# The order of a trunk kernel's last small operations, of its first casts and transposes, and of one low part of weights

## The chip, the cores and the metric

The kernel runs on one core of one Trainium2 chip. The metric is the time of one execution in microseconds (us) on the device. Five engines work in the core, each through its own list of instructions in order: TensorE (PE in the profile), VectorE (DVE), ScalarE (ACT), GpSimd (POOL) and SyncE (SP), which here only issues transfers.

## The reference, cut to what matters

One layer of a decoder trunk over 512 positions of 1024 values, all float32:

```python
u = rmsnorm(x, ln1_g)
proj = u @ w_in                                  # q, k, v, pool_in, z, xbc, dt, gates
y_a = dilated_attention_mixer(q, k, v, rel_bias) @ w_a
y_b = pool_mixer(pool_in, pool_w, pool_scale) @ w_b
y_c = ssd_mixer(z, xbc, dt, ...) @ w_c
x = x + (gates[0] * y_a + gates[1] * y_b + gates[2] * y_c) @ w_o
x = x + conv_ffn(rmsnorm(x, ln2_g), w_up, conv_w, conv_b, w_down)
return rmsnorm(x, final_g)
```

## The kernel before, in words

Matrix products are made from two parts of each operand, each in the type fp32r: a high part, which is a cast of the value, and a low part, which is the value less its high part. A product is three passes of matmuls: high by high, high by low and low by high. So each block of weights (`raw`) that has come from memory needs a cast into `wh` (ACT, `cast`, L195) and a subtraction into `wl` (DVE, `low`, L217) before its last pass. Weights come as a list of jobs. While job n is multiplied, `prepare` makes the low parts of job n+1, casts job n+2 and fetches job n+3. Every engine's order is the order in which the Python text issues its instructions.

Rows (positions) are kept in four blocks of 128, `tb` 0 to 3. Three places of the program matter here.

**The start.** x arrives in eight pieces, `xin[tb, h]`, h being the half of its 1024 values. `turned(tb)` (L1902) turns the eight 128x128 blocks k of a row block on PE into PSUM; for `tb` 0, 2 and 3 the blocks k and k+4 share a bank. `split_x(tb, k)` then makes `xh[k]` on ACT (L1906) and from it `xl[k]` on DVE (L1907). The first weights, `raw0`, come in two halves of 128 columns, j = 0 and 1. For j = 0 DVE makes the high part `h0` in two casts of 128x512 (L1952), which stand between the second and third `xl` of row block 1; GpSimd then makes the low part `l0` (`low0`, L1886). For j = 1 ACT makes the casts (L1959). On PE stand in a row: `group(0, (HH,))`, high by high for j = 0 over row blocks 0 and 1; `group(0, (HL,))`, with the low parts of x; `group(1, (HH,))`; `turned(2)`; `group(1, (HL,))`; `group(0, (LH,))`, which needs `l0` of j = 0; `turned(3)`; `group(1, (LH,))`, which needs `l0` of j = 1; and then the second half of the columns (all L1918). The build puts one more instruction, shown as `ISA` in the order, on GpSimd ahead of its first operation on two tensors; the profile shows it as two `MODIFY_POOL_CONFIG`.

**The opening of the feed-forward block.** The normed rows of row blocks 2 and 3 are not ready when the up products begin, so the first two up jobs (`opening`, L1560) multiply the first 256 columns alone, and the turns of row blocks 2 and 3 (`late`) lie between. `rest[0]` holds the steps of `prepare` for the first of these jobs: its first `next` makes the low parts of the second job's weights, its second one casts and fetches.

**The end.** `last_group` makes the last down products in seven jobs; the last, "A22", adds one half (512 columns) of row blocks 2 and 3. For each row block, `first` (L1631 on) takes the sum of squares of the half that is done earlier (`ss`) and makes of it the columns `v0` and `vh` on ACT (L1634, L1635). `gamma` multiplies that half by the final weights on DVE (L1641). When the other half has been read from its bank into x (L1694, DVE), `then` takes its sum of squares (ACT, L443) and a root (ACT, L1649), and the generator `rest` makes the norm's factor `rt` in four DVE operations of 128x1 (L1654 to L1657), multiplies both halves (DVE L1662, ACT L1663) and stores them (L1665). `go(tb)` runs `rest` to its next `yield`. The table `order` says which of these calls follow which reading:

```python
("A22", 0): [lambda: gamma(3, 1)],
("A22", 1): [lambda: go(2), lambda: go(2), lambda: go(3), lambda: go(3)]}
```

Of the kernel before, what the change touches and what calls it, by code (L numbers as in the profile page):

```python
# [12 lines left out]
AF = mybir.ActivationFunctionType  # L13
# [3 lines left out]
P = 128  # L17
S = 512
D = 1024
KD = D // P  # L20
# [62 lines left out]
def trunk(ctx: ExitStack, tc, out, x, rel_bias, ln1_g, w_in, b_gate, w_a, pool_w, pool_scale, w_b,  # L83
# [3 lines left out]
    act, dve, pool, pe, sp = nc.scalar, nc.vector, nc.gpsimd, nc.tensor, nc.sync  # L87
# [3 lines left out]
    out = out[0]  # L91
# [17 lines left out]
    def MM(name):  # L109
        return psum.tile([P, S], F32, name=name, tag="mm")  # L110

    def SM(name):
        return psum.tile([P, S], F32, name=name, tag="sm")
# [7 lines left out]
    eps = cpool.tile([P, 1], F32, name="eps")  # L121
# [121 lines left out]
    def chunk_a(ps, ws, j, xh, xl, ks, lo=0, hi=S, k0=0):  # L243
        wh, wl = ws
        mm3(ps[:, lo:hi], lambda k: wh[:, k0 + k, j * P:(j + 1) * P],
            lambda k: wl[:, k0 + k, j * P:(j + 1) * P],
            lambda k: xh(k)[:, lo:hi], lambda k: xl(k)[:, lo:hi], ks)
# [269 lines left out]
    bias = []  # L517
# [769 lines left out]
    COLS = [[cpool.tile([P, 1], F32, name=f"{n}{tb}") for n in ("so", "va", "vo")] for tb in range(4)]  # L1287
# [164 lines left out]
    def up_evac(m, ps):  # L1452
        t = HC[m] = T("hc")
        act.activation(t, ps, AF.Identity, bias=ff["c1"][:, ff["b"] + m:ff["b"] + m + 1], scale=fw(2, m))  # L1454
        for k in range(2):
            sh = 2 - k
            dve.scalar_tensor_tensor(t[:, sh:], ps[:, :S - sh], fw(k, m), t[:, sh:], OP.mult, OP.add)  # L1457
        if m < KF:
            act.activation(t, t, AF.Silu)  # L1459
            return  # L1460
        a = HC[m - KF]
        pool.tensor_tensor(a, a, t, OP.mult)  # L1462

        def later():
            yield
            k = m - KF
            if k % 2:
                h, l = T("fh", F32R), T("fl", F32R)
                act.copy(h, a)
                it = sums_of(HC[k - 1], a, T("sah", F32R), T("sal", F32R),  # L1470
                             lambda j, h, l: FS.__setitem__((j, k // 2), (h, l)), k >= KS)
                next(it)
                dve.tensor_sub(l, a, h.bitcast(F32))
                ACTS[k] = (h, l)
                yield
                for _ in it:
                    yield
                return
            t = T("f0", F32R)
            act.copy(t[:, :256], a[:, :256])  # L1480
            dve.tensor_sub(t[:, 256:], a[:, :256], t[:, :256].bitcast(F32))
            FS[0, k // 2] = (t[:, :256], t[:, 256:])

        running.append(later())
# [61 lines left out]
    def up_jobs():  # L1546
        held, rest = [], []

        def opening(job, half):
            def body(ws):  # L1550
                uh2, ul2 = nxt["uh"], nxt["ul"]
                if half == 0:
                    rest.append(job.prepare(later=True))
                    next(late[1])
                pss = [MM("pu") for _ in range(2)]

                def product(a, b, i):
                    for j in range(2):
                        for k in range(KD):
                            pe.matmul(pss[j][:, :256], a[:, k, j * P:(j + 1) * P], b[:, k, :256],  # L1560
                                      start=i + k == 0, stop=i == 2 and k == KD - 1)

                product(ws[0], uh2, 0)
                product(ws[0], ul2, 1)
                if half == 0:
                    product(ws[1], uh2, 2)
                next(late.pop(0), None)

                next(rest[0], None)
                if half:  # L1570
                    product(ws[1], uh2, 2)
                for j in range(2):
                    held.append((ws, j, pss[j], KF * half + j))
                if half == 0:
                    return
                for n, (ws_, j, ps, m) in enumerate(held):
                    chunk_a(ps, ws_, j, lambda k: uh2[:, k, :], lambda k: ul2[:, k, :], range(KD), 256, S)
                    if n == 1:
                        job.prepare()
                    up_evac(m, ps)  # L1580
                    step()
            return body

        for p in range(KF // 2):
            for half in range(2):
                def body(ws, p=p, half=half):
                    uh2, ul2 = nxt["uh"], nxt["ul"]
                    for j in range(2):
                        ps = MM("pu")
                        chunk_a(ps, ws, j, lambda k: uh2[:, k, :], lambda k: ul2[:, k, :], range(KD))  # L1590
                        up_evac(KF * half + 2 * p + j, ps)
                        step()
                c = half * DFF + p * 256
                job = Job([wsrc(w_up, 0, KD, c, c + 256)], KD, 256, body)
                if p == 0:
                    job.late = True
                    job.body = opening(job, half)
                yield job
# [3 lines left out]
    def last_group():  # L1602
# [22 lines left out]
        def begin():  # L1625
            fin["g"] = grow(final_g)
            act.activation(small("sq", [P, 1]), eps, AF.Sqrt)

        def first(tb, h):
            half = 1 - h  # L1630
            ss, v0, vh = COLS[tb]  # L1631
            xg = T("xg")
            squares(act, X1[tb, half], ss)
            act.activation(v0, ss, AF.Identity, bias=eps, scale=1.0 / D)  # L1634
            act.mul(vh, v0, -0.5)  # L1635
            fin[tb] = xg
            if tb < 2:
                pool.tensor_tensor(xg, X1[tb, half], fin["g"][half], OP.mult)

        def gamma(tb, half):  # L1640
            dve.tensor_tensor(fin[tb], X1[tb, half], fin["g"][half], OP.mult)  # L1641

        def then(tb, h):
            t, g = X1[tb, h], fin["g"]
            _, v0, vh = COLS[tb]
            ss, v, sq, r, rt = (small(n, [P, 1]) for n in ("ss", "v", "sq", "r", "rt"))
            o = {1 - h: fin[tb], h: T("xg")}
            squares(act, t, ss)
            act.activation(sq, ss, AF.Sqrt, bias=v0, scale=1.0 / D)  # L1649
            if tb < 2:  # L1650
                pool.tensor_tensor(o[h], t, g[h], OP.mult)

            def rest():
                dve.scalar_tensor_tensor(v, ss, -0.5 / D, vh, OP.mult, OP.add)  # L1654
                dve.reciprocal(r, sq)
                dve.scalar_tensor_tensor(rt, r, v, r, OP.mult, OP.mult)
                dve.scalar_tensor_tensor(rt, rt, 1.5, r, OP.add, OP.mult)  # L1657
                yield
                if tb < 2:
                    act.mul(o[h], o[h], rt)  # L1660
                else:
                    dve.scalar_tensor_tensor(o[h], t, rt, g[h], OP.mult, OP.mult)  # L1662
                act.mul(o[1 - h], o[1 - h], rt)  # L1663
                for i in (h, 1 - h):
                    (sp if i == h or tb < 3 else act).dma_start(  # L1665
                        out[tb * P:(tb + 1) * P, i * S:(i + 1) * S], o[i])
                yield

            fin["rest", tb] = rest()

        def go(tb):
            next(fin["rest", tb])
# [38 lines left out]
        def three_read(tb, h):  # L1711
            if tb == 0:
# [12 lines left out]
        order = {(2, 1): [lambda: go(0), lambda: go(0)],  # L1725
                 (3, 0): [lambda: go(1), lambda: seven.prepare(), lambda: go(1)],
                 (3, 1): [lambda: gamma(2, 1)],
                 ("A22", 0): [lambda: gamma(3, 1)],
                 ("A22", 1): [lambda: go(2), lambda: go(2), lambda: go(3), lambda: go(3)]}

        def soon():
            four.load = None
# [124 lines left out]
    raw0 = w0.raw = wraw.tile([P, KD, 256], F32, name="raw", tag="raw")  # L1857
# [19 lines left out]
    h0 = w0.high = whp.tile([P, KD, 256], F32R, name="wh", tag="wh")  # L1877
# [3 lines left out]
    def part(j, k0, k1):  # L1881
        return slice(None), slice(k0, k1), slice(j * P, (j + 1) * P)

    def low0(j, k0, k1):
        o = part(j, k0, k1)
        pool.tensor_tensor(l0[o], raw0[o], h0[o].bitcast(F32), OP.subtract)  # L1886
# [11 lines left out]
    def turned(tb):  # L1898
        if tb % 2 == 0:
            banks[:] = [SM("uT") for _ in range(4)]  # L1900
        for k in range(KD):
            pe.transpose(block(tb, k), xin[tb, k // 4][:, (k % 4) * P:(k % 4 + 1) * P], eye)  # L1902

    def split_x(tb, k):
# [31 lines left out]
    ss = small("ss", [P, 8])  # L1936
# [9 lines left out]
    for k in range(KD):  # L1946
        split_x(0, k)
    turned(1)
    for k in range(KD):
        if k == 2:  # L1950
            for k0 in (0, 4):
                dve.tensor_copy(h0[part(0, k0, k0 + 4)], raw0[part(0, k0, k0 + 4)])  # L1952
            low0(0, 0, KD)
        split_x(1, k)
    warm_up(STILL, 0)
    group(0, (HH,), 0, 256)
# [36 lines left out]
    rt, rd = T("rowsT"), dram.tile([S], F32, name="rows")  # L1993
# [86 lines left out]
```

## Time and profile before

| what | value |
|---|---|
| median of three runs | 1012.55 us (1012.4 to 1013.15) |
| the profiled execution | 1012.54 us, its span 1010.8 us |
| granted TensorE clock | 0.998 of full speed |
| PE busy | 999.7 us, 99% of the span |
| DVE busy | 753.7 us, 75% |
| ACT busy | 534.7 us, 53% |
| GpSimd busy | 137.8 us, 14% |

A timeline row gives start and length in us, engine, line, operation, what is written from what (buffer numbers left out), shapes and count, and in brackets how long the engine had been idle and what ended that. PEld is the loading of the stationary operand, which overlaps PE. A row with a q behind the engine's name belongs to the engine's sequencer. The chain that ended last is followed back from the last instruction, at each step to what released it.

### The profile page before, as it was taken

How to read it: one execution, taken by the hardware profiler on the slowest of the kernel's cores; microseconds unless marked ns; L12 is line 12 of the kernel's file. 1: busy time of each engine (PE TensorE's matmuls, PEld its weight loads, DVE VectorE, ACT ScalarE, POOL GpSimd, SP SyncE). 2: the span in 40 equal slices, each digit the busy share in tenths (PEclk: the TensorE clock that was granted, in tenths of full speed). 3: DMA queues.
4: the chain of work that ended last, by engine and by line, in shares of the span. 5: the costliest groups of instructions: out<-in, count | busy, mean ns of one | idle time of the engine just before them, and what ended most of it. 6: DMA issues, size and time to landing. Idle time of an engine off the chain costs nothing.

```text
span 1010.8 us, 13607 instructions
## 1 busy us (share of the span) xinstructions
PE 999.7 (99%) x5307; PEld 850.0 (84%) x5307; DVE 753.7 (75%) x962; ACT 534.7 (53%) x929; POOL 137.8 (14%) x111
## 2 busy tenths in 40 slices
PE   9999999999999999999999999999999999999996
PEld 8898878999988888888888888898888888888885
DVE  6995668677767645776889888868778768685877
ACT  6343546554445566888566246554444434443456
POOL 4400010110000000000044501302111100121032
PEclk9999999999999999999999999999999999999999
DMA  7344360755343435552254754232352134542573
GB/s 221 102 126 131 106 187 4 193 150 147 102 155 94 108 100 132 146 137 62 77 152 125 211 188 90 80 126 84 99 193 84 50 117 149 175 115 73 146 184 109
DMA packets 117735, 127.03 MB, mean 126 GB/s; under 512 B 6791, under 2 KB 96462, under 8 KB 117671
## 3 DMA queue, kind: packets, MB, share of 16 engines
q1 hardware_dynamic: 112327, 116.98, 37.4%
q0 software_dynamic: 5040, 8.65, 5.4%
q8 instruction: 42, 0.69, 0.3%
q10 hardware_dynamic: 304, 0.53, 0.1%
q14 instruction: 22, 0.18, 0.1%
HBM read 121.56 MB, written 3.00 MB: 123 GB/s over the span
## 4 chain that ended last, share of the span: by engine, by line
PE 96%; DVE 2%; ACT 0%; DMA 0%; issue 0%; ACTq 0%
PE pa L239 37%; PE pu L239 23%; PE pb L239 10%; PE pd L239 8%; PE pqk L239 6%; PE pq L239 3%; PE ps L810 1%; PE pa L1918 1%; PE ppw L239 1%; PE po L858 1%; PE pt L844 1%; PE py L1140 1%; DVE wl L217 1%; PE pyo L1147 1%; PE pst L1128 0%; DMA xin<-in_x_dram 0%
## 5 line engine op out<-in xcount | busy, mean ns | idle before, releaser
L217 DVE TENSOR_TENSOR wl<-raw,wh 128x2048 fp32r<-128x2048 f32 (+3 forms) x86 | 205.9, 2396 | 32.9 <-ACT wh L195 24.2
L195 ACT CAST wh<-raw 128x1024 fp32r<-128x1024 f32 (+2 forms) x168 | 167.0, 1011 | 53.0 <-DVE raw L362 17.8
L1457 DVE SCALAR_TENSOR_TENSOR hc<-pu,fcol,hc 128x510 f32<-128x510 f32 x88 | 65.9, 748 | 53.7 <-ACT hc L1454 52.0
L239 PE MATMUL pu<-uh,wh 128*128 128x512 f32 (+1 forms) x352 | 83.6, 379 | 0.0
L239 PE MATMUL pu<-uh,wl 128*128 128x512 f32 (+1 forms) x352 | 83.5, 379 | 0.0
L239 PE MATMUL pu<-ul,wh 128*128 128x512 f32 (+1 forms) x352 | 83.5, 379 | 0.0
L239 PE MATMUL pa<-uh,wh 128*128 128x512 f32 (+1 forms) x336 | 80.9, 380 | 0.0
L239 PE MATMUL pa<-ul,wh 128*128 128x512 f32 (+1 forms) x336 | 78.9, 374 | 0.0
L239 PE MATMUL pa<-uh,wl 128*128 128x512 f32 (+1 forms) x336 | 78.8, 374 | 0.0
L239 PEld LDWEIGHTS pu<-ul,wh 128*128 128x128 f32 x352 | 64.2, 188 | 12.5
L239 PEld LDWEIGHTS pu<-uh,wl 128*128 128x128 f32 x352 | 64.2, 188 | 12.4
L239 PEld LDWEIGHTS pu<-uh,wh 128*128 128x128 f32 x352 | 64.1, 188 | 12.4
L1454 ACT ACTIVATE hc<-pu,fcol,fcol 128x512 f32<-128x512 f32 x40 | 31.2, 779 | 75.7 <-PE pu L239 75.7
L239 PEld LDWEIGHTS pa<-ul,wh 128*128 128x128 f32 x336 | 60.7, 188 | 11.4
L239 PEld LDWEIGHTS pa<-uh,wl 128*128 128x128 f32 x336 | 60.7, 188 | 11.2
L239 PEld LDWEIGHTS pa<-uh,wh 128*128 128x128 f32 x336 | 59.4, 189 | 10.6
L1462 POOL TENSOR_TENSOR hc<-hc 128x512 f32<-128x512 f32 x22 | 29.9, 1360 | 279.0 <-DVE hc L1457 243.3
L217 DVE TENSOR_TENSOR wl<-w,wh 128x2048 fp32r<-128x2048 f32 (+1 forms) x26 | 54.3, 2088 | 9.8 <-issue 4.5
L195 ACT CAST wh<-w 128x1024 fp32r<-128x1024 f32 (+1 forms) x52 | 47.2, 950 | 8.6 <-DMA w<-in_ffn_w_down_dram 3.8
L832 ACT ACTIVATE sb<-sb,nmls 128x128 f32<-128x128 f32 (+1 forms) x72 | 30.0, 418 | 32.5 <-DVE nmls L829 21.9
L1459 ACT ACTIVATE hc<-hc 128x512 f32<-128x512 f32 x22 | 13.9, 633 | 40.3 <-DVE hc L1457 40.3
L1123 POOL TENSOR_TENSOR st<-st,dts 128x512 f32<-128x512 f32 x4 | 4.2, 1051 | 225.4 <-ACT st L1131 164.9
(461 smaller groups left out, 2012.8 us busy)
## 6 DMA issues: line engine op xcount, KB each, us to landing
raw<-in_w_in_dram SPq DMA_DIRECT2D x24, 1024.0 KB, 5.5
raw<-in_ffn_w_up_dram SPq DMA_DIRECT2D x22, 1024.0 KB, 5.1
raw<-in_w_in_dram SPq DMA_DIRECT2D x14, 512.0 KB, 4.0
raw<-in_w_in_dram SPq DMA_DIRECT2D x8, 768.0 KB
raw<-in_ffn_w_down_dram SPq DMA_DIRECT2D x6, 1024.0 KB, 4.9
raw<-in_w_b_dram SPq DMA_DIRECT2D x4, 1024.0 KB
al<-ad SPq DMA_DIRECT2D x16, 256.0 KB, 7.9
raw<-in_w_c_dram SPq DMA_DIRECT2D x4, 1024.0 KB, 5.3
```

Source lines behind the costliest of these rows:

```text
L195: (other.tensor_copy if other and i else act.copy)(job.high[:, :, o], job.raw[:, :, o])
L217: (eng or dve).tensor_tensor(l[:, :, o], job.raw[:, :, o], h[:, :, o].bitcast(F32), OP.subtract)
L239: pe.matmul(ps, l, r, start=first and n == 0, stop=last and n == total - 1, skip_group_check=onto)
L810: pe.matmul(pss[i][:, o:o + w * P], q[r, n * P:(n + 1) * P], k[r, kb * P:(kb + w) * P], start=True, stop=True)
L832: act.activation(sb[:, off:off + w * P], sb[:, off:off + w * P], AF.Exp, bias=nm[:, n, h:h + 1], accum_out=ls[:, n, h:h + 1])
L844: pe.transpose(pt[:, o:o + P], sb[:, o:o + P], eye)
L858: pe.matmul(po[DH * hh:DH * hh + DH, n * P:(n + 1) * P], V[g, kb + i][:, (2 * c + hh) * DH:(2 * c + hh + 1) * DH], probs[2 * c + hh, nb][: ...
L1140: pe.matmul(py[DH * i:DH * i + DH, j * P:(j + 1) * P], xc[:, o:o + DH], als[j // 2][:, lo:lo + P], start=True, stop=True)
L1454: act.activation(t, ps, AF.Identity, bias=ff["c1"][:, ff["b"] + m:ff["b"] + m + 1], scale=fw(2, m))
L1457: dve.scalar_tensor_tensor(t[:, sh:], ps[:, :S - sh], fw(k, m), t[:, sh:], OP.mult, OP.add)
L1459: act.activation(t, t, AF.Silu)
L1462: pool.tensor_tensor(a, a, t, OP.mult)
```

## The change

Four edits, and all but the last few operations on each engine keep their shapes and counts:

1. The two casts of `raw0`'s first half go from DVE to GpSimd, and all of them and `low0` are issued ahead of row block 1's `split_x`.
2. `turned` takes the blocks in the order 0, 4, 1, 5, 2, 6, 3, 7, bank by bank.
3. In `opening`, the low parts of the second up job are issued ahead of row block 3's norm (`next(late[1])`), where before they stood behind row block 2's turn.
4. At the end, row block 2's norm factor (`go(2)`) is issued ahead of the reading of row block 3's last bank, its product and stores in another order; row block 3's `v0` and `vh` go behind row block 2's sum of squares.

```diff
@@ opening
                     rest.append(job.prepare(later=True))
+                    next(rest[0])
                     next(late[1])
@@
                 next(late.pop(0), None)
 
-                next(rest[0], None)
                 if half:
+                    next(rest[0], None)
                     product(ws[1], uh2, 2)
@@ last_group
+        def columns_of_norm(tb):
+            ss, v0, vh = COLS[tb]
+            act.activation(v0, ss, AF.Identity, bias=eps, scale=1.0 / D)
+            act.mul(vh, v0, -0.5)
+
         def first(tb, h):
@@
-            act.activation(v0, ss, AF.Identity, bias=eps, scale=1.0 / D)
-            act.mul(vh, v0, -0.5)
+            if tb < 3:
+                columns_of_norm(tb)
@@ rest, after rt
                 if tb < 2:
                     act.mul(o[h], o[h], rt)
-                else:
+                    store(h)
+                act.mul(o[1 - h], o[1 - h], rt)
+                store(1 - h)
+                yield
+                if tb > 1:
                     dve.scalar_tensor_tensor(o[h], t, rt, g[h], OP.mult, OP.mult)
-                act.mul(o[1 - h], o[1 - h], rt)
-                for i in (h, 1 - h):
-                    (sp if i == h or tb < 3 else act).dma_start(
-                        out[tb * P:(tb + 1) * P, i * S:(i + 1) * S], o[i])
+                    store(h)
                 yield
@@ order
-                 ("A22", 0): [lambda: gamma(3, 1)],
-                 ("A22", 1): [lambda: go(2), lambda: go(2), lambda: go(3), lambda: go(3)]}
+                 ("A22", 0): [lambda: columns_of_norm(3), lambda: gamma(3, 1), lambda: go(2), lambda: go(2)],
+                 ("A22", 1): [lambda: go(2), lambda: go(3), lambda: go(3), lambda: go(3)]}
@@ turned
-        for k in range(KD):
+        for k in (0, 4, 1, 5, 2, 6, 3, 7):
@@ the start
     turned(1)
+    for k0 in (0, 4):
+        pool.tensor_copy(h0[part(0, k0, k0 + 4)], raw0[part(0, k0, k0 + 4)])
+    low0(0, 0, KD)
     for k in range(KD):
-        if k == 2:
-            for k0 in (0, 4):
-                dve.tensor_copy(h0[part(0, k0, k0 + 4)], raw0[part(0, k0, k0 + 4)])
-            low0(0, 0, KD)
         split_x(1, k)
```

GpSimd at the start of the program, before the change (`raw` is `raw0`, `wh` and `wl` are `h0` and `l0`):

```order
L2076 UNCONDITIONAL_BRANCH
L1886 ISA
L1886 TENSOR_TENSOR wl<-raw,wh 128x8x128 x2
L1973 TENSOR_TENSOR xf<-xh,xl 128x256 x8
L642 TENSOR_TENSOR xf<-xf,rows 128x512 x8
```

And the same place after it:

```order
L2086 UNCONDITIONAL_BRANCH
L1961 CAST wh<-raw 128x4x128 x2
L1897 ISA
L1897 TENSOR_TENSOR wl<-raw,wh 128x8x128 x2
L1983 TENSOR_TENSOR xf<-xh,xl 128x256 x8
L642 TENSOR_TENSOR xf<-xf,rows 128x512 x8
```

The two casts now stand first, and the `ISA` row, which stood first, stands behind them and ahead of the low parts.

DVE in the opening of the feed-forward block, the two as one piece of the difference (`va`, `vo`, `v`, `r`, `rt` are the columns of row block 3's norm, `u` its normed half, `ul` the low parts of the turned rows):

```order
 L1330 TENSOR_SCALAR va_106<-so_105 128x1
 L1331 TENSOR_SCALAR vo_107<-va_106 128x1
+L217 TENSOR_TENSOR wl<-raw,wh 128x2048
 L475 SCALAR_TENSOR_TENSOR v<-ss,vo_107 128x1
 L476 RECIPROCAL r<-sq 128x1
```

The low parts, which stood between the `ul` of row block 2 and of row block 3, now stand within row block 3's norm.

DVE at the end, before the change (`x_5513` and `x_5515` are the last halves of row blocks 2 and 3, each read from its bank `pb`):

```order
L1694 TENSOR_TENSOR x_5513<-x_5513,pb 128x512
L1641 TENSOR_TENSOR xg<-x_5678,grow 128x512
L1694 TENSOR_TENSOR x_5515<-x_5515,pb 128x512
L1654 SCALAR_TENSOR_TENSOR v<-ss,vo_104 128x1
L1655 RECIPROCAL r<-sq 128x1
L1656 SCALAR_TENSOR_TENSOR rt<-r,v 128x1
L1657 SCALAR_TENSOR_TENSOR rt<-rt,r 128x1
L1662 SCALAR_TENSOR_TENSOR xg<-x_5513,rt,grow 128x512
```

And after it:

```order
L1705 TENSOR_TENSOR x_5513<-x_5513,pb 128x512
L1647 TENSOR_TENSOR xg<-x_5678,grow 128x512
L1660 SCALAR_TENSOR_TENSOR v<-ss,vo_104 128x1
L1661 RECIPROCAL r<-sq 128x1
L1662 SCALAR_TENSOR_TENSOR rt<-r,v 128x1
L1663 SCALAR_TENSOR_TENSOR rt<-rt,r 128x1
L1705 TENSOR_TENSOR x_5515<-x_5515,pb 128x512
L1672 SCALAR_TENSOR_TENSOR xg<-x_5513,rt,grow 128x512
```

The four small operations of row block 2 have moved ahead of the reading of `x_5515`; the product behind them stays behind it.

More of the change, by code (lines that the diff above doesn't have):

```diff
@@ L1627, in begin @@
             act.activation(small("sq", [P, 1]), eps, AF.Sqrt)
+        def columns_of_norm(tb):
+            ss, v0, vh = COLS[tb]
+            act.activation(v0, ss, AF.Identity, bias=eps, scale=1.0 / D)
+            act.mul(vh, v0, -0.5)
         def first(tb, h):
             half = 1 - h
-            ss, v0, vh = COLS[tb]
+            ss = COLS[tb][0]
             xg = T("xg")
             squares(act, X1[tb, half], ss)
-            act.activation(v0, ss, AF.Identity, bias=eps, scale=1.0 / D)
-            act.mul(vh, v0, -0.5)
+            if tb < 3:
+                columns_of_norm(tb)
             fin[tb] = xg
@@ L1660, in rest, with store @@
                     act.mul(o[h], o[h], rt)
-                else:
+                    store(h)
[3 more added lines that the diff above has]
+                if tb > 1:
                     dve.scalar_tensor_tensor(o[h], t, rt, g[h], OP.mult, OP.mult)
-                act.mul(o[1 - h], o[1 - h], rt)
-                for i in (h, 1 - h):
-                    (sp if i == h or tb < 3 else act).dma_start(
-                        out[tb * P:(tb + 1) * P, i * S:(i + 1) * S], o[i])
+                    store(h)
                 yield
+            def store(i):
+                (sp if i == h or tb < 3 else act).dma_start(
+                    out[tb * P:(tb + 1) * P, i * S:(i + 1) * S], o[i])
             fin["rest", tb] = rest()
```

## The prediction

> **What bounds the kernel now.** I read the busy shares first, then the chain that ended last, by engine and then in order of time at the three places that the change touches.
>
> ```profile
> PE 999.7 (99%) x5307; PEld 850.0 (84%) x5307; DVE 753.7 (75%) x962; ACT 534.7 (53%) x929; POOL 137.8 (14%) x111
> PE 96%; DVE 2%; ACT 0%; DMA 0%; issue 0%; ACTq 0%
> ```
>
> PE is busy nearly always and carries the chain. So an edit pays only where PE waits, and what PE loses or gains at the start or in the middle goes through to the end. The chain in order of time, at the start:
>
> ```profile
> 1.36 4.20 DMA xin<-in_x_dram
> 5.61 0.78 PE uT L1902 x5
> 6.41 0.38 ACT xh L1906
> 6.81 2.68 DVE xl L1907 x10
> 9.49 0.67 DVE wh L1952 x2
> 10.16 0.27 DVE xl L1907
> 10.46 0.38 ACT xh L1906
> 10.88 2.80 PE pa L1918 x19
> ```
>
> Until 10.88 PE is not the bound. The chain goes through five transposes, ten `xl`, DVE's two casts, one more `xl` and an `xh`. From 10.88 on it is PE's. At the other two places the chain reads:
>
> ```profile
> 666.80 2.18 PE pu L1560 x16
> 668.99 98.59 PE pu L239 x480
> ...
> 1002.98 0.69 DVE x L1694
> ...
> 1005.67 0.75 DVE xg L1662
> ```
>
> In the opening PE begins its last pass at 666.80. At the end the last bank is read at 1002.98, and the last product starts 2.69 us later.
>
> **The start without its danger.** ACT's first `xh` comes behind the fifth transpose, the second and last block of bank 0. In the new order that block is the second. A run of eight takes this long:
>
> ```profile
> 13.52 1.04 PE L1902 MATMUL uT<-eye,xin 128*128 128x128 f32 x8
> 11.24 1.13 ACT L1959 CAST wh<-raw 128x512 fp32r<-128x512 f32 x2
> L1123 POOL TENSOR_TENSOR st<-st,dts 128x512 f32<-128x512 f32 x4 | 4.2, 1051 | 225.4 <-ACT st L1131 164.9 <-PE pst L1128 34.5 <-DVE xs L1153 26.1
> L1860 SPq DMA_DIRECT2D raw<-in_w_in_dram x2: 434/508/582, 2.6 to 3.1; - x2
> DMA to landing us min/median/max: 6.0/6.0/6.0
> ```
>
> Eight in 1.04 us is some 0.11 between starts (an estimate, the last one's length taken off), so three fewer are 0.33 us. The second half of x had landed, since the five run without a gap. Taking the casts off DVE lets the chain skip 0.67. Row block 1's split then ends 1.0 us earlier, near 10.35 by my count of its steps.
>
> GpSimd can begin its casts when the first weights land: 2.6 + 6.0 = 8.6. The trace has no GpSimd cast. DVE's two take 0.67 in the chain, 0.34 each, and GpSimd's two-input operation of the same size 1.05; these are the bounds of one cast. I take 0.65, nearest to ACT's cast of one input (1.13 for two). The casts end near 10.0, or at 10.8 with 1.05, when most of the gain would go. With 10.0, PE's first group ends 1.0 us earlier.
>
> ```profile
> 15.34 1.12 PE L1918 MATMUL pa<-xh,wl 128*128 128x256 f32 x8
> 16.30 1.35 PE L1902 MATMUL uT<-eye,xin 128*128 128x128 f32 x8
> 17.41 1.20 PE L1918 MATMUL pa<-xh,wl 128*128 128x256 f32 x8
> ```
>
> The turn of row block 3 took 1.35 here against 1.04 for row block 2, since it waited for `xl` of row block 2, which now comes earlier. That is another 0.3. So without the next point the start gives 1.3 us, and PE wants `l0` of j = 0 at 14.3 (15.34 less the first 1.0).
>
> **The danger.** GpSimd's `ISA` row, in the profile's words:
>
> ```profile
> L1886 POOLq MODIFY_POOL_CONFIG  x2: 11/11/11, 0.7 to 0.8; - x2
> L1886 POOL TENSOR_TENSOR wl<-raw,wh x2: 2398/2626/2853, 10.2 to 12.6; 128x1024 fp32r<-128x1024 f32 x2
> w<-in_w_in_dram POOLq DMA_DIRECT2D x8, 192.0 KB, 5.4
> w<-in_w_in_dram POOLq DMA_DIRECT2D x4, 256.0 KB, 7.2
> 14.00:15.00 1.00, 1.00 (x12) 1.00 (x10) 0.34 (x2) 0.74 (x3) 1.00 (x1) 1.00 1.09 345
> ```
>
> Before, the configuration is issued at 0.8 and the first two-input operation starts at 10.2, right behind DVE's casts. Whatever it sets off had 9.4 us under cover of GpSimd's waiting. After the change it stands behind the casts, so that cover is gone, and `l0` is queued behind it. What it costs is not in the trace. Its bounds are 0 and 9.4. If it brings something from memory, its nearest rows are GpSimd's own transfers from memory, 5.4 and 7.2 us. I take 7.2, as the DMA engines are full at that time (share 1.09, the last column but one, in 14 to 15). Then `l0` of j = 0 starts at 10.0 + 7.2 = 17.2, is done at 19.6 (2.40), and that of j = 1 at 22.0. PE, ready at 14.3, waits until 19.7, 5.4 us.
>
> [...]
>
> A wait of 5.4 us also touches the clock:
>
> ```profile
> 1006.00:1007.00 1.00, 0.00 (x0) 0.00 (x0) 0.42 (x1) 0.39 (x1) 0.00 (x0) 1.00 1.02 379
> 1007.00:1008.00 1.00, 0.00 (x0) 0.00 (x0) 0.00 (x0) 0.00 (x0) 0.00 (x0) 0.72 1.02 375
> ```
>
> PE's last matmul ended just ahead of 1002.98, and the granted clock (1.00 to 1007, 0.72 over the next microsecond) fell some 4.5 us later. So it should fall in this wait too. The group for j = 0 and the turn of row block 3 need 1.75 us at full clock (17.41 - 15.34, less the 0.3), and twice that at half: PE reaches the group for j = 1 at 19.7 + 3.5 = 23.2, behind `l0`'s 22.0. Against 17.41 that is 5.8 us later. Without the clock's fall it would be 22.0, 4.6 later. I keep the fall.
>
> [...]
>
> ACT's and DVE's steps for row block 3 hang on its turn and move with PE. What follows is again PE's, so I carry 5.8 us to the end.
>
> **The opening.**
>
> ```profile
> 660.31 0.15 DVE L1331 TENSOR_SCALAR vo<-va 128x1 f32<-128x1 f32 x1
> 661.98 0.75 DVE L482 SCALAR_TENSOR_TENSOR u<-x,rt,grow 128x512 f32<-128x512 f32 x1
> 664.47 2.28 DVE L217 TENSOR_TENSOR wl<-raw,wh 128x2048 fp32r<-128x2048 f32 x1
> 660.43 1.03 PE L457 MATMUL uT<-eye,u 128*128 128x128 f32 x8
> 661.22 2.15 PE L1560 MATMUL pu<-uh,wh 128*128 128x256 f32 x16
> 665.13 1.04 PE L457 MATMUL uT<-eye,u 128*128 128x128 f32 x8
> ```
>
> PE goes from a turn to the next pass in 661.22 - 660.43 = 0.79 us. Behind the second turn it could start at 665.92 but waits for the low parts, done at 666.75, and starts at 666.80. Moved to 660.4, they end at 662.7. That removes 0.88 us. The price: row block 3's `u` starts some 1.5 us later, at 663.5, and ends at 664.2, ahead of the turn at 665.13 that needs it. ACT's casts and the `ul` of row block 2 move behind it by as much, and PE does not read them before 667. So 0.9 us is kept; if that slack of 0.9 were gone, it would be nothing. The next raw buffer also comes free 4 us earlier, which moves SP's fetch and no wait of PE's.
>
> **The end.**
>
> ```profile
> 1001.91 0.62 ACT L443 ACTIVATE junk<-x 128x512 f32<-128x512 f32 x1
> 1002.65 0.29 ACT L1649 ACTIVATE sq<-ss,va 128x1 f32<-128x1 f32 x1
> 1003.65 0.16 DVE L1655 RECIPROCAL r<-sq 128x1 f32<-128x1 f32 x1
> 1004.29 0.75 DVE L1662 SCALAR_TENSOR_TENSOR xg<-x,rt,grow 128x512 f32<-128x512 f32 x1
> 1004.96 0.15 DVE L1654 SCALAR_TENSOR_TENSOR v<-ss,vo 128x1 f32<-128x1 f32 x1
> ```
>
> With two column operations behind it, row block 2's square sum on ACT starts 0.2 earlier and its root ends near 1002.7, not 1002.94. Then `r` to the end of `rt` takes 0.61 on DVE (1003.65 to 1004.26). The last bank is read at about 1003.3: 0.3 later. But the chain from there to the last product no longer has row block 2's four operations in it, which held row block 3's `v` until 1004.96 where its sum of squares was there at 1004.4: some 0.26 less. Together 0 to 0.1 us slower. Row block 2's stores go out 0.8 us earlier, ahead of the last two. I take 0, between -0.3 and +0.3.
>
> **The sum.** +5.8 - 0.9 + 0 = +4.9 us on the profiled execution's 1012.54 us (span 1010.8 and 1.74 around it; the median of the runs is 1012.55): 1017.4 us.
>
> **The rivals.** *The configuration costs nothing where it now stands* (what it wants is already there): then -1.3 - 0.9 + 0 = -2.2, 1010.3 us, faster. For it speaks that the issue itself takes 11 ns and that no transfer of it is seen; against it, that the row stands ahead of the first two-input operation and that nothing limits what it did before 10.2. It decides below 1.9 us: 10.0 + 1.9 + 2.4 = 14.3, when PE asks. *It is short*, 2 to 5.5 us: at 4, `l0` of j = 1 is done at 18.8, 1.4 behind the old 17.41, the clock does not fall, and the sum is +0.5, 1013.0 us. *The cast is as dear as a two-input operation*, at no load: PE's first group gains little, and some 0.7 us is left to the start's 0.3: -1.0 to -1.2, 1011.4 us, no change that counts. *The load is as long as it can have been*, 9.4: +2.2 on the forecast, 1019.6 us.
>
> **How the numbers follow.** A measurement of this kernel tells 0.2%, 2.0 us, from no change. The forecast's case (a load of 5.5 to 9.4 us) has 0.66: it alone is read as a mechanism that the move takes out of its cover. Its own range is 1014.7 to 1019.6. No load has 0.22, half of it beyond 2.0 us: 0.11 faster, 0.11 the same. The short load has 0.07 and the dear cast 0.05, both the same. So faster 0.11, same 0.23, slower 0.66. The range takes in the no-load case, 1010.3, and the longest load, 1019.8.
>
> **What would show it.** In the changed profile, `MODIFY_POOL_CONFIG` near 10 with the first GpSimd `TENSOR_TENSOR` 5 us or more behind the casts' end, PE's longest wait of the program ahead of L1929's `pa<-xh,wl`, ended by POOL, and a clock below 1.00 in a stretch near 20. If that gap is under 2 us, the forecast is wrong and its first rival right. The opening is right if no wait for `wl` stands ahead of the second L1561 pass with `wl`, and the end if reading to last product takes about 2.4 us.

## The result, and the profile after

The changed kernel takes 1010.64 us (median of 13 runs, 1010.38 to 1011.28), the kernel before in the same session 1012.88 (13 runs, 1011.96 to 1013.46). The ratio is 0.998, with a 95% interval of 0.9973 to 0.9987: 2.24 us faster, where 4.9 us slower was forecast. The profiled executions have spans of 1010.8 us before and 1008.8 us after.

Lines of the changed kernel stand some ten further down than those of before: L1886 is now L1897, L1902 is L1913, L1918 is L1929, L1952 is L1961, L1694 is L1705, L1662 is L1672. The busy shares, from the page of the changed kernel:

```profile
PE 999.1 (99%) x5307; PEld 849.9 (84%) x5307; DVE 754.4 (75%) x960; ACT 534.8 (53%) x929; POOL 139.4 (14%) x113
```

PE has the same instructions. Of the 2.0 us that the span lost, 0.6 lie in PE's busy time, in which short waits inside a group of matmuls count (row block 3's turn takes 1.04 us below where it took 1.35), and the rest in its idle time; so what was gained is waiting. The configuration, on which the forecast hung, from the view of GpSimd's line of two-input operations (counts, then shortest, median and longest duration in ns, then first and last start in us) and from GpSimd's timeline:

```profile
L1897 POOLq MODIFY_POOL_CONFIG  x2: 11/11/11, 9.9 to 10.0; - x2
L1897 POOL TENSOR_TENSOR wl<-raw,wh x2: 2409/2632/2854, 10.1 to 12.4; 128x1024 fp32r<-128x1024 f32 x2
...
8.84 1.17 POOL L1961 CAST wh<-raw 128x512 fp32r<-128x512 f32 x2 [8.39 <-DMA raw<-in_w_in_dram]
10.08 5.22 POOL L1897 TENSOR_TENSOR wl<-raw,wh 128x1024 fp32r<-128x1024 f32 x2
```

The casts end at 10.0 as forecast, the configuration stands right behind them as forecast, and the first two-input operation starts at 10.08, some 0.1 us later, where 7.2 us had been put in. PE's timeline of the start:

```profile
9.50 1.29 PE L1929 MATMUL pa<-xh,wh 128*128 128x256 f32 x8 [0.33 <-POOL wh L1961]
...
14.37 1.12 PE L1929 MATMUL pa<-xh,wl 128*128 128x256 f32 x8
15.33 1.04 PE L1913 MATMUL uT<-eye,xin 128*128 128x128 f32 x8
16.12 1.20 PE L1929 MATMUL pa<-xh,wl 128*128 128x256 f32 x8
...
22.93 2.09 PE L239 MATMUL pa<-xh,wh 128*128 128x512 f32 x8
```

Neither group with `wl` waits. The one for j = 1 starts at 16.12, 1.29 us ahead of the old 17.41. The last row is the program's first full-width product, L239; in the kernel before it starts at 24.22 (quoted below), so the whole 1.29 us is kept. The chain in order of time shows what bounds the start now:

```profile
2.60 6.18 DMA raw<-in_w_in_dram
...
8.84 0.62 POOL wh L1961
```

It was DVE's `xl` and casts; it is now the landing of the first weights and GpSimd's first cast. The opening and the end, from the timelines of PE and of DVE:

```profile
664.60 2.15 PE L1561 MATMUL pu<-uh,wl 128*128 128x256 f32 x16
...
999.87 0.85 PE L239 MATMUL pb<-wl,fh 128*128 128x512 f32 x3
...
1001.07 0.68 DVE L1705 TENSOR_TENSOR x<-x,pb 128x512 f32<-128x512 f32 x1
...
1003.52 0.75 DVE L1672 SCALAR_TENSOR_TENSOR xg<-x,rt,grow 128x512 f32<-128x512 f32 x1
```

The pass of the opening has no bracket: PE no longer waits ahead of it, and it starts 2.20 us earlier than the old 666.80, 1.3 from the start and 0.9 from its own wait. At the end PE's last matmul ends at 1000.72, the last bank is read at 1001.07 and the last product starts at 1003.52, 2.15 us ahead of before. The chain goes another way there than it did:

```profile
1001.18 0.72 ACT xg L1668
1001.90 0.62 ACT junk L443 x2
```

It no longer runs through PE's last matmul and the reading. ACT first scales a half of row block 2, and by the chain row block 3's sum of squares follows that at 1001.90, 0.15 us behind the end of the reading (1001.07 + 0.68).

### The profile page after: what moved, and what is told of

The parts are those of the page before. It is cut to its first block, busy times and chain, and to the rows that moved or that the text cites. A ratio compares the mean times of both kernels' runs of the same rounds, so it can differ in the third digit from the quotient of the medians.

```text
span 1008.8 us, 13607 instructions
## 1 busy us (share of the span) xinstructions
PE 999.1 (99%) x5307; PEld 849.9 (84%) x5307; DVE 754.4 (75%) x960; ACT 534.8 (53%) x929; POOL 139.4 (14%) x113
## 4 chain that ended last, share of the span: by engine, by line
PE 97%; DVE 1%; DMA 1%; ACT 0%; SPq 0%; issue 0%; POOL 0%
PE pa L239 37%; PE pu L239 23%; PE pb L239 11%; PE pd L239 8%; PE pqk L239 6%; PE pq L239 3%; PE ps L810 1%; PE pa L1929 1%; PE pu L1561 1%; PE ppw L239 1%; PE po L858 1%; PE pt L844 1%; PE py L1140 1%; DMA raw<-in_w_in_dram 1%; PE pyo L1147 1%; PE pst L1128 0%
## 5 line engine op out<-in xcount | busy, mean ns | idle before, releaser
L239 PE MATMUL pu<-uh,wh 128*128 128x512 f32 (+1 forms) x352 | 83.5, 379 | 0.0
L239 PE MATMUL pu<-uh,wl 128*128 128x512 f32 (+1 forms) x352 | 83.5, 379 | 0.0
L239 PE MATMUL pu<-ul,wh 128*128 128x512 f32 (+1 forms) x352 | 83.5, 379 | 0.0
L239 PE MATMUL pa<-uh,wh 128*128 128x512 f32 (+1 forms) x336 | 80.9, 380 | 0.0
L239 PE MATMUL pa<-ul,wh 128*128 128x512 f32 (+1 forms) x336 | 78.9, 374 | 0.0
L239 PE MATMUL pa<-uh,wl 128*128 128x512 f32 (+1 forms) x336 | 78.8, 374 | 0.0
L239 PEld LDWEIGHTS pu<-uh,wl 128*128 128x128 f32 x352 | 64.2, 188 | 12.5
L239 PEld LDWEIGHTS pu<-ul,wh 128*128 128x128 f32 x352 | 64.2, 188 | 12.5
L239 PEld LDWEIGHTS pu<-uh,wh 128*128 128x128 f32 x352 | 64.1, 188 | 12.4
L239 PEld LDWEIGHTS pa<-ul,wh 128*128 128x128 f32 x336 | 60.7, 188 | 11.4
L239 PEld LDWEIGHTS pa<-uh,wl 128*128 128x128 f32 x336 | 60.7, 188 | 11.2
L239 PEld LDWEIGHTS pa<-uh,wh 128*128 128x128 f32 x336 | 59.4, 189 | 10.6
L217 DVE TENSOR_TENSOR wl<-w,wh 128x2048 fp32r<-128x2048 f32 (+1 forms) x26 | 54.2, 2086 | 10.2 <-issue 4.5
```

The source lines that it names most:

```text
L217: (eng or dve).tensor_tensor(l[:, :, o], job.raw[:, :, o], h[:, :, o].bitcast(F32), OP.subtract)
L239: pe.matmul(ps, l, r, start=first and n == 0, stop=last and n == total - 1, skip_group_check=onto)
```

## The experiments

Three theories of the configuration were open after the result. *It never costs anything.* *It loads something, but what this kernel asks for is still there from the execution before*, so nothing is loaded. *A part of a load still lay in the start*, hidden by the casts. The first four runs bear on them.

**switch**: another kind of GpSimd operation at the start, so that two different configurations stand in the program.

```diff
     dve.memset(warm, 1.0)
+    far, near = small("far", [P, 4]), small("near", [P, 4])
+    pool.memset(far, 1.0)
+    pool.partition_broadcast(near, far)
```

> The changed kernel with one more GpSimd operation of another kind at the program's start, a broadcast of 128x4 over the partitions (a scratch result that nothing reads), for which the build puts a configuration of its own ahead of it and a second one ahead of the first two-input operation, behind the casts. If a configuration never costs anything, both gaps are about 0.1 us and the time is the changed kernel's. If it costs nothing only where what it asks for is already there, the second one, behind the casts, is now paid: a gap of some us between it and the first two-input operation, PE waiting ahead of the group with l0, and a time of the forecast's kind, +2 to +8 us on the changed kernel.

Measured: 1019.77 us, 1.0064 of the kernel before (1.0051 to 1.0078). From the views of the two lines, and then the rows of GpSimd's and PE's timelines:

```profile
L1860 POOLq MODIFY_POOL_CONFIG  x2: 11/11/11, 1.0 to 1.0; - x2
L1860 POOL PARTITION_BROADCAST near<-far x1: 282/282/282, 8.0 to 8.0; - x1
...
L1900 POOLq MODIFY_POOL_CONFIG  x2: 11/11/11, 10.0 to 10.0; - x2
...
18.27 4.65 POOL L1900 TENSOR_TENSOR wl<-raw,wh 128x1024 fp32r<-128x1024 f32 x2 [8.29 <-issue]
...
20.65 2.07 PE L1932 MATMUL pa<-xh,wl 128*128 128x256 f32 x8 [6.13 <-POOL wl L1900]
22.52 1.91 PE L1916 MATMUL uT<-eye,xin 128*128 128x128 f32 x8
...
31.03 2.09 PE L239 MATMUL pa<-xh,wh 128*128 128x512 f32 x8
```

Both are paid: 7.0 us from the first configuration (1.0) to the broadcast (8.0), 8.2 from the second (10.0) to `wl` (18.27). The idle time is put down to "issue", that is, to nothing that the profile shows. PE waits 6.13 us for it. The clock, from the table of 1 us windows (granted clock in the last column but two):

```profile
17.00:18.00 1.00, 0.00 (x0) 0.00 (x0) 0.00 (x0) 0.00 (x0) 0.00 (x0) 0.78 0.37 99
18.00:19.00 1.00, 0.00 (x0) 0.00 (x0) 0.00 (x0) 0.00 (x0) 0.73 (x1) 0.50 0.00 0
...
24.00:25.00 1.00, 1.00 (x9) 1.00 (x8) 0.83 (x3) 0.90 (x4) 1.00 (x3) 0.81 0.80 157
```

It falls in the wait, stands at 0.50 from 18 to 24 and is back at 1.00 from 25 to 29 (0.81 in the microsecond before), and the group and the turn behind the wait take 2.07 and 1.91 us where they took 1.12 and 1.04. L239 starts 8.1 us later than in the changed kernel. So a configuration can cost what the forecast said, by a wait and a fall of the clock as it had them, with gaps of 7.0 and 8.2 us where it had taken 7.2; the first theory is out.

**lib**: the same operation at the changed kernel's end and none at its start.

```diff
     finish()
+    far = small("far", [P, 4])
+    pool.memset(far, 1.0)
+    near = small("near", [P, 4])
+    pool.partition_broadcast(near, far)
```

> The changed kernel with the broadcast of 128x4 (a scratch result that nothing reads) at the program's end and none at its start, so that an execution of it leaves the other configuration behind and begins with the one on two tensors, behind the casts. If what the first configuration asks for was left by the execution before, an execution that follows one of this kernel pays some 8 us between the configuration and the first two-input operation at the start, and takes some 1019 us. If each execution begins with it anew, the gap at the start stays 0.1 us, and only the broadcast at the end pays its own, some 7 us behind its configuration, beside the last stores: less than that is added to the time, and the profile shows which.

Measured: 1019.33 us, 1.0066 (1.0043 to 1.0089); all three executions took 1018.7 us or more. From the views of the lines, and the timelines:

```profile
L1897 POOLq MODIFY_POOL_CONFIG  x2: 13/13/13, 10.3 to 10.3; - x2
...
19.05 4.66 POOL L1897 TENSOR_TENSOR wl<-raw,wh 128x1024 fp32r<-128x1024 f32 x2 [8.75 <-issue]
...
32.13 2.08 PE L239 MATMUL pa<-xh,wh 128*128 128x512 f32 x8
```

Up to 19.05 its program is the changed kernel's, instruction for instruction, yet now the gap is 8.7 us and L239 starts 9.2 us later than in the changed kernel, about as much as the whole run is longer (span 1017.9 against 1008.8). The added operation comes too late to cost this in its own execution. So, as I read it, what the configuration asks for outlives an execution, and in the changed kernel it costs nothing because that kernel uses one kind alone and finds it in place.

One rival of this reading was not tested: that a program with one kind has it in place from when the program is loaded, and that a program with two kinds pays at every configuration, whatever the execution before left. switch and lib fit that too. A program with the same kind first and last and another kind between would tell the two apart. Nor do the runs record which kernel was executed directly ahead of each execution.

**oldlib**: the same lines at the end of the kernel before.

> The kernel before with the broadcast of 128x4 (a scratch result that nothing reads) at its end, as the run lib put it behind the changed kernel. lib showed that what a configuration asks for is kept from the execution before, and that it costs 8.7 us when it is not there. In the kernel before the first configuration is issued at 0.8 us and the first two-input operation waits until 10.2 for DVE's casts, so a load of 7 to 8.7 us lies under cover: the theory that only the lost cover makes it cost asks for the kernel before's own time within 0.3 us. If a load costs its time wherever it stands, this is 7 to 9 us slower, as lib is.

Measured: 1014.23 us, 1.0013 (1.0004 to 1.0022). Its configuration, GpSimd's timeline and PE's:

```profile
L1886 POOLq MODIFY_POOL_CONFIG  x2: 11/11/11, 0.8 to 0.8; - x2
...
10.25 5.20 POOL L1886 TENSOR_TENSOR wl<-raw,wh 128x1024 fp32r<-128x1024 f32 x2 [9.82 <-DVE wh L1952]
...
24.24 2.09 PE L239 MATMUL pa<-xh,wh 128*128 128x512 f32 x8
...
L2044 POOLq MODIFY_POOL_CONFIG  x2: 11/11/11, 1004.4 to 1004.5; - x2
...
1010.19 0.28 POOL near L2044
```

The start is that of the kernel before, 24.24 against 24.22. The load that by the reading of lib was due here (the expectation takes that reading as shown; the rival above is open too) shows in no row; it fits under the wait until 10.2, as the prediction had said of the old place. The 1.5 us come from the other end: the last row, from its chain, shows the added broadcast itself as the last to finish, 5.7 us behind its configuration. I had expected it to be hidden there. So moving the configuration behind the casts did take away a cover of some 9 us. In the changed kernel nothing lay under it: the gap behind the casts is 0.1 us there.

**early**: the changed kernel with the configuration back at the program's start.

```diff
     dve.memset(warm, 1.0)
+    two = small("two", [P, 1])
+    pool.tensor_tensor(two, warm, warm, OP.add)
```

> The changed kernel with one more GpSimd operation on two 128x1 columns at the program's start (a scratch result that nothing reads), so that MODIFY_POOL_CONFIG is issued at about 0.8 us again, under the wait for the first weights. If the configuration costs nothing, this runs as the changed kernel does, within 0.1 us, and the gap ahead of the first two-input operation on weights is the same 0.1 us. If a part of a load still lay in the start of the changed kernel, this one is faster by that part, and its wl starts sooner behind the casts.

Measured: 1010.58 us, 0.998 (0.9971 to 0.9989), the changed kernel's time. Its configuration and GpSimd's timeline:

```profile
L1859 POOLq MODIFY_POOL_CONFIG  x2: 11/11/11, 0.7 to 0.8; - x2
...
1.26 0.19 POOL L1859 TENSOR_TENSOR two<-warm 128x1 f32<-128x1 f32 x1 [0.82 <-DVE relb L526]
...
8.41 1.17 POOL L1963 CAST wh<-raw 128x512 fp32r<-128x512 f32 x2 [6.95 <-DMA raw<-in_w_in_dram]
9.66 5.20 POOL L1899 TENSOR_TENSOR wl<-raw,wh 128x1024 fp32r<-128x1024 f32 x2
```

The added operation starts at 1.26, half a microsecond behind its configuration, when DVE lets it go (the bracket). So with no long wait to cover it, too, no gap of microseconds followed. From the casts' end (9.58) to `wl` it is 0.1 us again. No part of a load was hidden in the changed kernel, and the third theory is out.

**start, opening, end**: each the kernel before with the edits at one place alone, as the diff of the change shows them.

> The kernel before with both edits at the start (GpSimd's two casts, the turns bank by bank) and nothing else. The forecast's theory, a load of 5.5 to 9.4 us behind the configuration once it stands behind the casts, asks for +4 to +8 us on the kernel before, with 5 us or more between MODIFY_POOL_CONFIG and the first GpSimd TENSOR_TENSOR. The theory that I hold now, that the configuration costs nothing where it stands because what it wants is already there, asks for -1.3 us (PE's last group of the start, L239's first row behind it, 1.3 us earlier than 24.22) and a gap of some 0.1 us between the two.

> The kernel before with the edit in the opening alone (low parts of the second up job ahead of row block 3's norm). My step: -0.9 us, the wait for wl ahead of the second pass at 666.80 gone, and all else as before. The rival, that row block 3's later norm holds its turn on PE, asks for a gap ahead of that turn and -0.9 turned into less, down to 0.

> The kernel before with the edit at the end alone. My step: 0, within 0.3 us either way: the last bank is read some 0.3 us later behind PE's end, and from there to the last product it takes some 2.4 us and not 2.69. The rival, that the shorter chain is all that counts, asks for -0.3 us with the bank read right behind PE's end, as before; the other one, that row block 2's operations hold the reading without a return, for +0.3 us.

Measured against 1012.66 us of the kernel before: start 1011.37 (ratio 0.9987, 0.9979 to 0.9996), -1.3 us; opening 1011.56 (0.9990, 0.9981 to 0.9999), -1.1; end 1012.85 (1.0002, 0.9993 to 1.0011), no difference that can be told. Together -2.2, which is what all four edits gave at once. PE's timelines, first of the kernel with the start alone, then of the one with the opening alone:

```profile
22.89 2.08 PE L239 MATMUL pa<-xh,wh 128*128 128x512 f32 x8
```

```profile
665.50 1.04 PE L457 MATMUL uT<-eye,u 128*128 128x128 f32 x8
666.29 2.15 PE L1561 MATMUL pu<-uh,wl 128*128 128x256 f32 x16
```

In the opening alone the pass follows the turn after 0.79 us, the distance of an undisturbed turn, where it was 1.67 (666.80 - 665.13): 0.88 us gone. And of the end alone, PE's last matmuls and DVE's reading and last product:

```profile
1001.92 0.84 PE L239 MATMUL pb<-wl,fh 128*128 128x512 f32 x3
...
1003.14 0.68 DVE L1704 TENSOR_TENSOR x<-x,pb 128x512 f32<-128x512 f32 x1
...
1005.59 0.75 DVE L1671 SCALAR_TENSOR_TENSOR xg<-x,rt,grow 128x512 f32<-128x512 f32 x1
```

PE ends at 1002.76, the reading starts 0.38 later, the last product 2.45 behind it, where the kernel before has 2.69 from reading to product: as the step said, nothing won.

**casts and banks**: the two edits of the start taken apart, one execution each.

> The kernel before with GpSimd's two casts and low0 ahead of row block 1's split, the turns in their old order. My step: the chain loses DVE's 0.67 us of casts and PE's first group waits for the xl and xh behind the fifth transpose, so PE's later rows of the start (L239's first one, 24.22 before) come some 0.7 to 1.0 us earlier; MODIFY_POOL_CONFIG stands near 10.0 with the first two-input operation 0.1 us behind it.

> The kernel before with the turns bank by bank and DVE's casts where they were. My step: 0.33 us at most, the first xh some 0.3 us earlier, and DVE's casts then wait for the landing of the first weights, near 8.8, so that a part of it may go. The rival, that the order of the turns carries most of what the start gained, asks for over 0.7 us.

Measured: casts 1011.95 us, banks 1012.65, each from one run, against 1012.77. The rows of PE's timeline, of casts first, then L239 of the kernel before, then of banks:

```profile
15.60 1.35 PE L1902 MATMUL uT<-eye,xin 128*128 128x128 f32 x8
...
23.52 2.09 PE L239 MATMUL pa<-xh,wh 128*128 128x512 f32 x8
```

```profile
24.22 2.09 PE L239 MATMUL pa<-xh,wh 128*128 128x512 f32 x8
```

```profile
5.83 1.81 PE L1902 MATMUL uT<-eye,xin 128*128 128x128 f32 x9
...
16.75 1.04 PE L1902 MATMUL uT<-eye,xin 128*128 128x128 f32 x8
...
24.35 2.09 PE L239 MATMUL pa<-xh,wh 128*128 128x512 f32 x8
```

GpSimd's casts alone bring 0.70 us, and with the order of the banks as well 1.33 (22.89 in the kernel with both), by one execution of each. Row block 3's turn takes 1.35 with the casts alone, as before, and 1.04 with the order of the banks. For banks alone the first turn was disturbed: nine transposes took 1.81 us, where the changed kernel has nine in 1.20. So this execution can't say what the order brings by itself at the first turn.

**best and stores**: can the end be had cheaper? In best, row block 2's `v` and `r` alone stand ahead of the last reading.

```diff
                 dve.reciprocal(r, sq)
+                if tb > 1:
+                    yield
...
-                 ("A22", 0): [lambda: columns_of_norm(3), lambda: gamma(3, 1), lambda: go(2), lambda: go(2)],
-                 ("A22", 1): [lambda: go(2), lambda: go(3), lambda: go(3), lambda: go(3)]}
+                 ("A22", 0): [lambda: columns_of_norm(3), lambda: gamma(3, 1), lambda: go(2)],
+                 ("A22", 1): [lambda: go(2), lambda: go(2), lambda: go(2)] + [lambda: go(3)] * 4}
```

> The changed kernel with row block 2's v and r alone ahead of the reading of the last bank, and its two rt, its products and stores behind it. DVE is idle for some 0.35 us between gamma and those two operations in the changed kernel's profile, so the reading should start right behind PE's end, 0.3 us earlier; from the reading to the last product 2.45 us stays, if row block 2's rt, rt and product (some 1.2 us) fit in ahead of row block 3's sum of squares (there 1.5 us behind the reading's start). Together 0.2 to 0.3 us less than the changed kernel, some 1010.4 us. If they do not fit, the chain grows back and nothing is gained.

Measured: 1010.93 us, 0.9982 (0.9973 to 0.9991). Its chain at the end:

```profile
999.95 0.92 PE pb L239 x4
...
1000.89 0.69 DVE x L1707
...
1003.34 0.75 DVE xg L1674
```

The step came out, the gain did not. The chain goes through the reading again, with the reading right behind PE's end and the last product 2.47 us after that end (1003.34 - 1000.87), where the changed kernel has 2.80. But from the last product's start to the end of the span (1009.0) it is 5.66 us, against 5.28 there. The run after it swaps row block 2's two products and their stores:

```diff
+                if tb == 2:
+                    dve.scalar_tensor_tensor(o[h], t, rt, g[h], OP.mult, OP.mult)
+                    store(h)
                 act.mul(o[1 - h], o[1 - h], rt)
                 store(1 - h)
                 yield
-                if tb > 1:
+                if tb == 3:
```

> The kernel of the run best with row block 2's last product and its store ahead of its other half's scaling and store. In best the last product came 0.31 us sooner behind PE's end than in the changed kernel, and the tail from its start to the end of the span was 0.4 us longer; row block 2's two stores were issued back to back there, ahead of row block 3's. If that order of the stores is what gave the gain back, the tail is some 5.3 us again and the time 0.3 us below the changed kernel's, about 1010.3 us. If the tail is set by the stores' landing in any case, nothing changes.

Measured: 1010.19 us, 0.9974 (0.9963 to 0.9984), the fastest of all. From its timeline:

```profile
23.61 2.09 PE L239 MATMUL pa<-xh,wh 128*128 128x512 f32 x8
...
1003.83 0.75 DVE L1677 SCALAR_TENSOR_TENSOR xg<-x,rt,grow 128x512 f32<-128x512 f32 x1
```

From the last product's start to the end of the span (1009.0) it is 5.17 us, short again. L239 starts 0.68 us later in this execution than in the changed kernel's (23.61 against 22.93), since PE's first transposes were slow in it (the last section). So the stretches are compared from L239's first row to the span's end: 985.39 us here, 985.87 in the changed kernel, 985.89 in best. That is 0.48 us won by these rows, 0.45 by the medians; the intervals of the two kernels' ratios overlap, so the gain over the changed kernel rests on the rows of one execution each, not on the times. Which transfer held the tail in best stays open.

## Why the prediction was wrong

- **The danger: this step failed.** "I take 7.2" put a load behind the moved configuration. Measured: 0.1 us between the configuration and `wl`, no wait of PE ahead of either group with `wl`, and a granted clock of 1.00 in every microsecond from 3 to 27. The bounds, 0 and 9.4, held the answer, and the first rival had it with its number: 1010.3 us against 1010.64. What failed was the weighing. The prediction asked where the load would lie and how long it would be, and left to a rival of 0.22 the question whether anything had to be loaded. lib shows what that question decides: the same first two-input operation behind the same configuration starts after 0.1 us in the changed kernel and after 8.7 there. Whether what the configuration asks for is in place from the execution before or from the loading of a program with one kind stays open, as said at lib; either way the term was nothing here.
- **What the danger would have cost** was near: with another kind left behind, 8.7 us of load in lib and 8.2 in switch where 7.2 was taken, in switch a wait of PE of 6.1 us where 5.4 was taken and the clock at 0.50 where half was forecast, and 9.2 and 8.1 us behind the changed kernel at L239, where the forecast had 7.1 between its case and the one without a load (5.8 against -1.3). No row that the prediction quotes has the half; the kernel before shows it too, 0.50 in every window from 1008 to its end. The clock of switch fell sooner than the 4.5 us of the prediction: by the 0.78 of the window from 17 to 18 near 17.6 (an estimate), some 3.0 us behind the end of PE's matmuls at 14.52. oldlib fits a load covered at the old place. Two slips of the working changed nothing: the two `wl` take 5.2 us together (10.2 to 12.6, and 2853 ns of the second), not twice 2.40, so `l0` of j = 1 would have been done at 22.4 and not 22.0, still ahead of PE's 23.2; and the longest load stands as 1019.6 in one place and 1019.8 in another.
- **The start without its danger**: -1.3 forecast, -1.29 in the changed profile and -1.33 in the run of the start alone. Its parts came too: a cast took 0.61 us (0.65 taken, from 0.34 to 1.05 open), the casts alone brought 0.70 (0.67 taken), and the turn of row block 3 its 0.3. The reason given for that turn, that row block 2's `xl` come earlier, fits the timelines: the last of them ends 0.52 us behind the turn's start in the kernel before and in casts, where the turn takes 1.35, and 0.20 in the changed kernel, where it takes 1.04. What the prediction didn't say is that the order of the banks brings this: in banks the turn takes 1.04 too, and ACT's first `xh` follows the start of row block 2's turn by 0.74 us in the first two kernels and by 0.41 in the changed one. The same order also asks for the last bank three transposes later, some 0.33 us by the prediction's 0.11; the two were not taken apart.
- **The opening**: -0.9 forecast, -0.88 in the opening alone by the distance from turn to pass. No wait of row block 3's `u` took its place.
- **The end**: 0 forecast, as 0.3 later and 0.26 shorter. Measured in the changed kernel: the reading 0.35 behind PE's end where it was 0.04, and 2.45 to the last product where it was 2.69, together 0.07 us. The number held and the path only nearly: the prediction kept the chain on the reading, and in the changed kernel it runs through row block 2's scaling on ACT, 0.15 us behind.

## What to carry to other kernels

Here a configuration of GpSimd was followed by 5.7 to 8.7 us of waiting in the programs with a second kind of operation (switch, lib, the end of oldlib), by no more than the 9.8 us of waiting for DVE's casts at the start of oldlib, and by 0.1 us behind the casts in those with one kind (the rows of GpSimd's casts and memsets show no configuration in this kernel). By the reading of lib, what the execution before left counts too. So, on what these runs show, count the kinds of GpSimd operations in the whole program, its end included, before pricing one. With one kind, the place of the configuration was free: 1010.58 us in early against 1010.64. With two, as in switch and lib, a change of kind is better placed under a wait of that length. And where a term decides the sign, first ask what would have to be true for it to be zero, and price that as carefully as the size.

## What the runs showed of the hardware

- The load is nowhere in the busy time: in switch and lib the gap is idle time of GpSimd with "issue" as what ended it, and the configuration's own rows take 11 to 13 ns. No transfer shows it either: the pages of lib and of the changed kernel list the same packets and bytes for every DMA queue but one, an instruction queue with 23 packets against 22. So that it is a load is read from when the gap comes; it isn't seen. It took 7.0 and 8.2 us in switch and 8.7 us in lib at the start, 5.7 us at the end of oldlib and, from the rows below, 5.8 us at the end of lib. What sets the length stays open.

```profile
L2054 POOLq MODIFY_POOL_CONFIG  x2: 11/11/11, 1010.6 to 1010.6; - x2
...
L2054 POOL PARTITION_BROADCAST near<-far x1: 284/284/284, 1016.4 to 1016.4; - x1
```

- PE's first transposes differed in rate at a granted clock of 1.00 in the rows: nine in 1.81 us in banks at 5.83, nine in 1.20 at 5.25 in the changed kernel. The row below is of the windows of banks: six transposes in a microsecond in which PE is always busy, where the same window of the kernel before has twelve matmuls. The run stores has it too (nine in 1.74 us at 5.82). The matmuls of L1854 just ahead of them show more: the first twenty take 4.63 us in banks and 3.85 in the kernel before, and fourteen of the same shape that follow the transposes take 1.73 in both. So PE starts slow in both executions and comes to the later rate at different times, in banks only during these transposes. Why the time differs stays open, and the granted clock, 1.00 in both in every microsecond from 3 to 9, doesn't show it.

```profile
6.00:7.00 1.00, 1.00 (x6) 1.00 (x7) 0.15 (x2) 0.39 (x2) 0.00 (x0) 1.00 1.12 347
```
